# Reordering the modulation of the first norm in a two-sublayer decoder trunk

## The chip, the cores and the metric

The kernel runs on one core of one Trainium2 chip. The metric is the device time of one execution in microseconds, the median of several runs. TensorE is called PE here, VectorE DVE, ScalarE ACT, GpSimd POOL, and SP is the engine whose queue issues the DMAs.

## What is computed

One decoder layer on 1024 tokens of width 1024, in float32. A mixer sub-layer (three groups of heads) is followed by a gated feed-forward sub-layer and a final norm. Each sub-layer begins with an RMS norm that is scaled and shifted by a modulation: six vectors of 1024 that come from one product of the conditioning vector with a 1024 x 6144 matrix. The change is in the first of them.

```python
c_act = jax.nn.silu(c)
mod = c_act @ w_mod[l] + b_mod[l]
sh1, sc1, gt1, sh2, sc2, gt2 = [m[:, None, :] for m in jnp.split(mod, N_MOD, axis=-1)]
h = rms_norm(x, norm_mix[l]) * (1.0 + sc1) + sh1
p = h @ w_in[l]
...
x = x + gt1 * y
h = rms_norm(x, norm_ffn[l]) * (1.0 + sc2) + sh2
x = x + gt2 * conv_glu_ffn(h, ...)
return rms_norm(x, norm_final)
```

## The kernel before

Activations lie transposed: 128 of the 1024 channels on the partitions (a k tile, eight of them), 512 tokens along the free axis (a half f, two of them). A float32 product is made of three matmuls of a rounded format: a value is split into a high part `h` and a remainder `l` (ACT casts the high part, DVE or POOL subtracts for the remainder, `split` at L230), and h·h, h·l and l·h are summed.

**The stage around the change** (L411 to L454) makes h for the first 512 tokens. Its modulation comes in four groups m = 0 to 3; group m gives the shift and scale of the k tiles 2m and 2m+1 of h. A group's weights are four DMAs of 512 KB (`mod_load`, L336), tiles `wm` with two k tiles of 512 columns each. The product with the conditioning vector `cs` is spread over the engines: each of the eight k tiles is multiplied by its column of `cs` and added up. `mod_ap` (L343) does k 0 to 3: ACT multiplies, POOL adds, into the first sum `mb[m][0]`. `mod_v` (L350) does k 4 to 7 on DVE into the second sum `mb[m][1]`: one TENSOR_SCALAR and three SCALAR_TENSOR_TENSORs. `mod_fin` (L358) has PE sum both over the partitions (four one-column matmuls for each, tile `pm`), and DVE writes the result to `modc` (shift and scale) and `sg1` (scale plus one, times the norm's weight). Then `h_hi` (L372) multiplies x by `sg1` and by `rb`, the reciprocal root mean square of each token, and ACT adds the shift for the high part; `h_lo` (L380) is DVE's remainder. For k 0 to 3 DVE does both products at once; for k 4 to 7 POOL multiplies by `rb` (`xr`, L384) and DVE by `sg1`.

PE's products of the stage are three column tiles of the input projection, `pf0` to `pf2`; their weights `ws[0]` to `ws[2]` are split beside the modulation (`wh_s`, `wl_s`; the last remainder on POOL). Each takes 8 k tiles x 3 matmuls. `prod` (L400) emits those whose operands exist.

The order of the work is the order of the code, held fixed on DVE, ACT and POOL in this stage (`V.on`, `A.on`, `G.on`), and on PE while `T.on` is set. Before, group m's turn of the loop runs: ACT's and POOL's part of group m+1, the first two of DVE's four of group m+1, POOL's `xr`, `mod_fin(m)`, the matmuls of the first m weight tiles, `h_hi` of two k tiles, DVE's other two of group m+1, `h_lo`, and the split of weight tile m. An engine does its queue in order and waits at the first instruction that isn't ready.

After the stage ACT reads `pf0`, `pf1` and `pf2` (tiles `xwa`, `sgg`, `k`), PE goes on with the next column tile `pc_r`, and a chain of some 25 tiny operations (`spt`, L465 to L479) on POOL is followed there by `lol` (L490), which PE's product `pa` (L570) needs.

Of the kernel before, what the change touches and what calls it, by code (L numbers as in the profile page):

```python
# [10 lines left out]
F32 = mybir.dt.float32  # L11
# [7 lines left out]
P = 128  # L19
# [35 lines left out]
NF2 = 3  # L55
NT2, NTB, _ = 7, 9, 5
NWR, NWL, NH = 3, 2, 16
NAP, NXV, NFIRST, TON, XRO = (4, 4, 4, 4), 4, 3, True, ((4, 4), (4, 6), (6, 8), (8, 8))
VPIN = 0
ENG = {'s2':'G','KB1': 'V',  # L60
 'S1': 'V',
# [91 lines left out]
def trunk(ctx: ExitStack, tc: tile.TileContext, xT, wmod, w_in, w_out, w_up, w_down,  # L153
# [168 lines left out]
    def h_tile(f, k, x, rb, hl):  # L322
# [5 lines left out]
        V.scalar_tensor_tensor(lo, x, sh, hi.bitcast(F32), ALU.add, ALU.subtract)  # L328
        return hl

    acts = [[], []]
    first = {}
    with tc.tile_pool(name="st", bufs=1, reuse_waits="tile") as st:
        xs, ws = [], []

        def mod_load(m):  # L336
            for k2 in range(KT // 2):
                wt = st.tile([P, 2, H], F32, tag="wm", name=f"wm{m}_{k2}", bufs=6)
                SY.dma_start(wt, wmod[m, k2])
                wm[m] += [wt[:, 0, :], wt[:, 1, :]]  # L340
            mb[m] = [st.tile([P, H], F32, tag=f"mb{i}", name=f"mb{m}{i}", bufs=2) for i in range(2)]

        def mod_ap(m):  # L343
            a = mb[m][0]
            for k in range(NAP[m]):
                A.activation(wm[m][k] if k else a, wm[m][k], AF.Copy, scale=cs[:, k:k + 1])
                if k:
                    G.tensor_tensor(a, a, wm[m][k], ALU.add)

        def mod_v(m, k0, k1):  # L350
            a = mb[m][1]
            for k in range(max(k0, NAP[m]), k1):
                if k == NAP[m]:
                    V.tensor_scalar(a, wm[m][k], cs[:, k:k + 1], None, ALU.mult)
                else:
                    V.scalar_tensor_tensor(a, wm[m][k], cs[:, k:k + 1], a, ALU.mult, ALU.add)

        def mod_fin(m):  # L358
            ps = mp.tile([P, H], F32, tag="m", name=f"pm{m}")
            for n, a in enumerate(mb[m]):  # L360
                for i in range(4):
                    T.matmul(ps[:, i:i + 1], a[:, i * P:(i + 1) * P], ones, start=(n == 0 and i == 0), stop=(n == 1),
                             skip_group_check=True)
            V.tensor_tensor(modc[:, 4 * m:4 * m + 4], ps[:, 0:4], col("b_mod", 4 * m, 4), ALU.add)
            V.scalar_tensor_tensor(sg1[:, 2 * m:2 * m + 2], modc[:, 4 * m + 1:4 * m + 4:2], 1.0,
                                   col("norm_mix", 2 * m, 2), ALU.add, ALU.mult)

        def w_load(i):
            raw, hi, lo = ws[i]
            SY.dma_start(raw, w_in[i].rearrange("p k c -> p (k c)"))  # L370

        def h_hi(k):  # L372
            x, sh = xs[k], modc[:, 2 * k:2 * k + 1]
            if k < NXV:
                V.scalar_tensor_tensor(x, x, sg1[:, k:k + 1], rb, ALU.mult, ALU.mult)
            else:
                V.tensor_scalar(x, x, sg1[:, k:k + 1], None, ALU.mult)
            A.activation(hs[k][0], x, AF.Identity, bias=sh)

        def h_lo(k):  # L380
            V.scalar_tensor_tensor(hs[k][1], xs[k], modc[:, 2 * k:2 * k + 1], hs[k][0].bitcast(F32),
                                   ALU.add, ALU.subtract)

        def xr(k0, k1):  # L384
            for k in range(k0, k1):
                G.tensor_tensor(xs[k], xs[k], rb, ALU.mult)

        wm, mb = [[] for _ in range(4)], [None] * 4
        hs = [htile(f"h0{k}") for k in range(KT)]
        acts[0] += hs  # L390
        for i in range(NFIRST):
            raw = wp.tile([P, 1024], F32, tag="wraw", name=f"wr_s{i}", bufs=NWR)
            hi = st.tile([P, 1024], F32R, tag=f"wsh{i}", name=f"wh_s{i}")
            lo = st.tile([P, 1024], F32R, tag=f"wsl{i}", name=f"wl_s{i}")
            ws.append((raw, hi, lo))
            first[i] = acp.tile([P, H], F32, tag="acc", name=f"pf{i}")

        done = [0] * NFIRST

        def prod(k1, i1):  # L400
            for k in range(k1):
                ah, al = hs[k]
                for i in range(min(i1, NFIRST)):
                    if done[i] == k:
                        hi, lo = (t.rearrange("p (k c) -> p k c", c=P)[:, k, :] for t in ws[i][1:])
                        T.matmul(first[i], hi, ah, start=(k == 0), stop=False)
                        T.matmul(first[i], hi, al, start=False, stop=False)
                        T.matmul(first[i], lo, ah, start=False, stop=(k == KT - 1))
                        done[i] += 1

        V.on = A.on = G.on = True  # L411
        sacc = st.tile([P, H], F32, name="sacc0")
        for k in range(KT):
            xk = st.tile([P, H], F32, tag=f"x{k}", name=f"x0{k}")
            SY.dma_start(xk, xT[k * P:(k + 1) * P, 0:H])
            sq = st.tile([P, H], F32, tag="sq", name=f"sqx{k}", bufs=2)
            A.activation(sacc if k == 0 else sq, xk, AF.Square)
            if k:
                V.tensor_tensor(sacc, sacc, sq, ALU.add)
            xs.append(xk)  # L420
        mod_load(0)
        mod_load(1)
        mod_ap(0)
        rb = sumsq_bcast([sacc], mp, st, "rb", "n10", 1)
        mod_v(0, 0, 8)
        w_load(0)
        mod_load(2)
        w_load(1)
        mod_load(3)
        if NFIRST == 3:  # L430
            w_load(2)
        SY.dma_start(cst, const[:, 0:C_ID])
        lraw = wp.tile([P, 1024], F32, tag="wraw", name="lraw", bufs=NWR)[:, 0:768]
        SY.dma_start(lraw, lora.rearrange("p a b -> p (a b)"))
        for m in range(4):
            if m < 3:
                mod_ap(m + 1)
                mod_v(m + 1, 0, 6)
            xr(*XRO[m])
            T.on = TON  # L440
            mod_fin(m)
            if TON:
                prod(2 * m, m)
            T.on = False
            h_hi(2 * m)
            h_hi(2 * m + 1)
            if m < 3:
                mod_v(m + 1, 6, 8)
            h_lo(2 * m)
            h_lo(2 * m + 1)  # L450
            if m < NFIRST:
                split(*ws[m], eng(f"s{m}", "V"))
        prod(KT, NFIRST)
        V.on = A.on = G.on = False  # L454

# [32 lines left out]
    for i in range(2):  # L488
        r_, c_ = slice(64 * i, 64 * i + 64), slice(384 * i, 384 * i + 384)
        G.tensor_tensor(lol[r_, c_], lraw[r_, c_], lor[r_, c_].bitcast(F32), ALU.subtract)  # L490
    for i in range(NR):
        for t in (KGd, SCd, STd):
            G.memset(t[i], 0.0)
        if i < 2:
            G.memset(AKd[i][:, 0:4], 0.0)
            G.memset(AKd[i][:, 4:8], 0.0)
    g2s = r2.tile([P, 384], F32, name="g2s")
    SY.dma_start(g2s, g2w)
    lrw = r2.tile([P, 768], F32, name="lrw")
# [907 lines left out]
```

## Time and profile before

| | before |
|---|---|
| median of 3 runs | 1378.88 us (1377.09 to 1379.15) |
| the profiled execution, its own time | 1379.3 us |
| its span | 1377.5 us |
| PE busy | 1255.0 us (91% of the span) |
| DVE busy | 896.3 us (65%) |
| ACT busy | 583.7 us (42%) |
| POOL busy | 335.8 us (24%) |

The span is what the profiler sees of the program, the time is that of the execution around it. Busy time includes time in which an instruction has started and waits for something inside the engine, so a long DVE row can be a short one that was held up. The profile's chain of waits names only its longest pieces, the first of them at 747 us; for the first 75 us the engines' instructions are read one by one, in order of time.

### The profile page before, as it was taken

How to read it: one execution, taken by the hardware profiler on the slowest of the kernel's cores; microseconds unless marked ns; L12 is line 12 of the kernel's file. 1: busy time of each engine (PE TensorE's matmuls, PEld its weight loads, DVE VectorE, ACT ScalarE, POOL GpSimd, SP SyncE). 2: the span in 40 equal slices, each digit the busy share in tenths (PEclk: the TensorE clock that was granted, in tenths of full speed). 3: DMA queues.
4: the chain of work that ended last, by engine and by line, in shares of the span. 5: the costliest groups of instructions: out<-in, count | busy, mean ns of one | idle time of the engine just before them, and what ended most of it. 6: DMA issues, size and time to landing. Idle time of an engine off the chain costs nothing. (4 is left out here: it accounts for less than half of the span.)

```text
span 1377.5 us, 18630 instructions
## 1 busy us (share of the span) xinstructions
PE 1255.0 (91%) x6948; PEld 1026.9 (75%) x6948; DVE 896.3 (65%) x1667; ACT 583.7 (42%) x1008; POOL 335.8 (24%) x294
## 2 busy tenths in 40 slices
PE   3778999888998979999979899999999999999996
PEld 3566878667686767778757788888888888888885
DVE  6778765755668484467697766666566575432566
ACT  4364655854655366333363333434434342110231
POOL 6674423206125220000001433332333200000000
PEclk9899999979999997899998999999999999999998
DMA  7453251433314243296413322232222374321213
GB/s 283 156 169 100 56 165 54 120 117 85 83 48 112 63 121 116 86 301 204 129 61 99 100 82 72 84 92 84 91 67 81 126 249 138 88 78 52 80 54 122
DMA packets 87498, 153.89 MB, mean 112 GB/s; under 512 B 37616, under 2 KB 39280, under 8 KB 87408
## 3 DMA queue, kind: packets, MB, share of 16 engines
q1 hardware_dynamic: 87408, 152.71, 35.6%
q8 instruction: 54, 0.88, 0.3%
q14 instruction: 36, 0.29, 0.1%
HBM read 126.60 MB, written 26.08 MB: 111 GB/s over the span
## 5 line engine op out<-in xcount | busy, mean ns | idle before, releaser
L1249 DVE SCALAR_TENSOR_TENSOR x<-pd,modc,x 128x512 f32<-128x512 f32 x80 | 59.6, 749 | 85.4 <-PE pd L251 85.3
L290 POOL TENSOR_TENSOR macc<-macc,wm 128x512 f32<-128x512 f32 x35 | 47.1, 1345 | 67.9 <-ACT wm L288 65.7
L231 ACT CAST wh_wd<-wr_wd 128x768 fp32r<-128x768 f32 (+2 forms) x32 | 21.7, 678 | 95.9 <-PE pd L250 94.0
L1202 POOL TENSOR_TENSOR wr_uv<-wr_uv 128x512 f32<-128x512 f32 x3 | 4.5, 1516 | 227.4 <-DVE wr_ub L1201 227.4
L1296 POOL TENSOR_TENSOR x<-x,rb_n 128x512 f32<-128x512 f32 x2 | 3.0, 1515 | 217.3 <-ACT rb_n L273 217.3
L232 DVE TENSOR_TENSOR wl_ug<-wr_ug,wh_ug 128x1024 fp32r<-128x1024 f32 x22 | 26.9, 1224 | 38.9 <-ACT wh_ug L231 38.7
L1227 POOL TENSOR_TENSOR u<-u,g 128x512 f32<-128x512 f32 x21 | 27.7, 1321 | 92.8 <-ACT g L1150 92.8
L758 DVE TENSOR_SCALAR U<-q,rn 128x64 f32<-128x64 f32 x48 | 13.4, 279 | 48.9 <-PE q L746 41.7
L231 ACT CAST wh_ug<-wr_ug 128x1024 fp32r<-128x1024 f32 x22 | 23.2, 1054 | 48.3 <-PE pA L1125 35.6
L627 PE MATMUL pg<-KGd,KB 128*128 128x128 f32 x192 | 31.4, 309 | 8.4 <-DVE KGd L612 6.0
L766 ACT COPY O<-q 128x64 f32<-128x64 f32 x48 | 10.1, 210 | 66.4 <-PE q L746 66.1
L746 PE MATMUL q<-SS,KGd 128*128 128x64 f32 x180 | 37.2, 291 | 0.0
L1211 DVE TENSOR_TENSOR p<-p,pB 128x512 f32<-128x512 f32 x21 | 14.4, 686 | 34.9 <-PE pB L1126 34.9
L746 PE MATMUL q<-VV,SCd 128*128 128x64 f32 x192 | 35.5, 289 | 0.2
L627 PEld LDWEIGHTS pg<-KGd,KB 128*128 128x128 f32 x192 | 27.4, 216 | 9.9 <-DVE KGd L612 6.7
L1150 ACT ACTIVATE g<-g 128x512 f32<-128x512 f32 x44 | 27.9, 634 | 13.1 <-DVE g L1145 13.1
L746 PEld LDWEIGHTS q<-VV,SCd 128*128 128x128 f32 x192 | 30.3, 205 | 3.9 <-issue 1.1
L1143 DVE SCALAR_TENSOR_TENSOR g<-p,pr,g 128x511 f32<-128x511 f32 (+1 forms) x42 | 33.2, 790 | 0.0
L1143 DVE SCALAR_TENSOR_TENSOR g<-pA,pr,g 128x511 f32<-128x511 f32 (+1 forms) x42 | 31.2, 744 | 2.9 <-ACT g L1141 2.6
L288 ACT ACTIVATE wm<-wm,cs 128x512 f32<-128x512 f32 x35 | 24.1, 719 | 15.9 <-DMA wm<-in_wmod_dram 14.1
L1204 POOL TENSOR_TENSOR wr_ug<-wr_ug,wr_uv 128x512 f32<-128x512 f32 x18 | 29.9, 1663 | 1.4
L746 PEld LDWEIGHTS q<-SS,KGd 128*128 128x128 f32 x180 | 29.7, 207 | 0.5 <-issue 0.5
(5035 smaller groups left out, 4446.3 us busy)
## 6 DMA issues: line engine op xcount, KB each, us to landing
wm<-in_wmod_dram SPq DMA_DIRECT2D x48, 512.0 KB, 4.1
wr_ug<-in_w_up_dram SPq DMA_DIRECT2D x22, 512.0 KB, 3.6
wr_uv<-in_w_up_dram SPq DMA_DIRECT2D x22, 512.0 KB, 3.6
wr_g<-gd SPq DMA_DIRECT2D x22, 512.0 KB, 3.3
x<-in_xT_dram SPq DMA_DIRECT2D x32, 256.0 KB, 5.5
wr_wo<-in_w_out_dram SPq DMA_DIRECT2D x16, 512.0 KB, 4.2
wr_wd<-in_w_down_dram SPq DMA_DIRECT2D x16, 384.0 KB, 3.1
gd<-c SPq DMA_DIRECT2D x21, 256.0 KB, 2.0
```

Of the source, the lines that this page charges most:

```text
L231: A.copy(hi, src)
L232: (e or V).tensor_tensor(lo, src, hi.bitcast(F32), ALU.subtract)
L288: A.activation(acc if k == 0 else wt[:, j, :], wt[:, j, :], AF.Copy, scale=cs[:, k:k + 1])
L290: G.tensor_tensor(acc, acc, wt[:, j, :], ALU.add)
L627: T.matmul(pg[hh][:, c, :, :], KB[:, 4 * g + c, :, :].rearrange("p a b -> p (a b)"), KG[g][:, c, :, r_], start=True, stop=True)
L746: T.matmul(o, w, x, start=start, stop=True, skip_group_check=True)
L1143: V.scalar_tensor_tensor(g[:, d:H], src[:, 0:H - d], taps[2 - d], g[:, d:H], ALU.mult, ALU.add)
L1150: A.activation(g, g, AF.Silu)
L1204: eng("S4" + e, "G").tensor_tensor(g1, g1, v1, ALU.subtract)
L1211: V.tensor_tensor(self.p1, self.p1, psB, ALU.add)
L1227: eng("c22", "V").tensor_tensor(u3, u3, g1_, ALU.mult)
L1249: V.scalar_tensor_tensor(x, ps, modc[:, 40 + k:41 + k], x, ALU.mult, ALU.add)
```

## The change

The modulation is taken further ahead of h. ACT and POOL do the k tiles 1, 3 and 5 of each group, DVE does 0, 2, 4, 6 and 7 in one go. Groups 0 and 1 are done before the loop; in turn m ACT and POOL do group m+2, and DVE does group m+2 behind the two `h_lo` of group m and ahead of the split of weight tile m. `mod_fin(m+1)` stands between `h_hi` and `h_lo` of group m. POOL multiplies all eight k tiles by `rb`, and ACT takes DVE's product with `sg1`. The weights get eight buffers instead of six, and the zeroing of the rings (tiles `KGd`, `SCd`, `STd`, `AKd` of a later stage) moves to the top of the code.

```diff
-NAP, NXV, NFIRST, TON, XRO = (4, 4, 4, 4), 4, 3, True, ((4, 4), (4, 6), (6, 8), (8, 8))
+NFIRST = 3
+KAP_, KV_ = (1, 3, 5), (0, 2, 4, 6, 7)
...
+    for i in range(NR):
+        for t in (KGd, SCd, STd):
+            G.memset(t[i], 0.0)
+        if i < 2:
+            G.memset(AKd[i][:, 0:4], 0.0)
+            G.memset(AKd[i][:, 4:8], 0.0)
...
-                wt = st.tile([P, 2, H], F32, tag="wm", name=f"wm{m}_{k2}", bufs=6)
+                wt = st.tile([P, 2, H], F32, tag="wm", name=f"wm{m}_{k2}", bufs=8)
...
-            for k in range(NAP[m]):
-                A.activation(wm[m][k] if k else a, wm[m][k], AF.Copy, scale=cs[:, k:k + 1])
-                if k:
+            for k in KAP_:
+                first_ = k == KAP_[0]
+                A.activation(a if first_ else wm[m][k], wm[m][k], AF.Copy, scale=cs[:, k:k + 1])
+                if not first_:
                     G.tensor_tensor(a, a, wm[m][k], ALU.add)
...
-            for k in range(max(k0, NAP[m]), k1):
-                if k == NAP[m]:
+            for k in KV_[k0:k1]:
+                if k == KV_[0]:
...
-            if k < NXV:
-                V.scalar_tensor_tensor(x, x, sg1[:, k:k + 1], rb, ALU.mult, ALU.mult)
-            else:
-                V.tensor_scalar(x, x, sg1[:, k:k + 1], None, ALU.mult)
+            A.activation(x, x, AF.Copy, scale=sg1[:, k:k + 1])
...
-        mod_ap(0)
-        rb = sumsq_bcast([sacc], mp, st, "rb", "n10", 1)
-        mod_v(0, 0, 8)
...
+        mod_ap(0)
+        T.on = True
+        rb = sumsq_bcast([sacc], mp, st, "rb", "n10", 1)
+        T.on = False
+        mod_v(0, 0, 5)
+        fin(0)
+        mod_ap(1)
+        xr(0, 2)
+        mod_v(1, 0, 5)
         for m in range(4):
-            if m < 3:
-                mod_ap(m + 1)
-                mod_v(m + 1, 0, 6)
-            xr(*XRO[m])
-            T.on = TON
-            mod_fin(m)
-            if TON:
-                prod(2 * m, m)
-            T.on = False
+            if m + 2 < 4:
+                mod_ap(m + 2)
             h_hi(2 * m)
             h_hi(2 * m + 1)
-            if m < 3:
-                mod_v(m + 1, 6, 8)
+            if m + 1 < 4:
+                fin(m + 1)
+                xr(2 * m + 2, 2 * m + 4)
             h_lo(2 * m)
             h_lo(2 * m + 1)
+            if m + 2 < 4:
+                mod_v(m + 2, 0, 5)
             if m < NFIRST:
                 split(*ws[m], eng(f"s{m}", "V"))
+            T.on = True
+            prod(2 * m + 2, m + 1)
+            T.on = False
```

`fin(m)` is `mod_fin(m)` with PE's order held.

The change moves instructions on three engines; PE's and SP's orders stay. First DVE around the end of group 2 (`mb21` is DVE's sum of group 2, `mb31` that of group 3, `pm2` PE's sum of group 2 over the partitions, `wl_s0` and `wl_s1` the remainders of the first two weight tiles). Before:

```order
L149 TENSOR_TENSOR wl_s0_144<-wr_s0_142,wh_s0_143 128x1024
L149 TENSOR_SCALAR mb21_262<-wm2_2_257,cs_79 128x512
L149 SCALAR_TENSOR_TENSOR mb21_262<-wm2_2_257,cs_79,mb21_262 128x512
L149 TENSOR_TENSOR modc_76<-pm1_319,pr_66 128x4
L149 SCALAR_TENSOR_TENSOR sg1_77<-modc_76,pr_66 128x2
L149 SCALAR_TENSOR_TENSOR x02_164<-x02_164,sg1_77,rb_n10_246 128x512
L149 SCALAR_TENSOR_TENSOR x03_169<-x03_169,sg1_77,rb_n10_246 128x512
L149 SCALAR_TENSOR_TENSOR mb21_262<-wm2_3_259,cs_79,mb21_262 128x512 x2
L149 SCALAR_TENSOR_TENSOR h02l_131<-x02_164,modc_76,h02h_130 128x512
L149 SCALAR_TENSOR_TENSOR h03l_133<-x03_169,modc_76,h03h_132 128x512
L149 TENSOR_TENSOR wl_s1_148<-wr_s1_146,wh_s1_147 128x1024
L149 TENSOR_SCALAR mb31_273<-wm3_2_268,cs_79 128x512
```

With the change:

```order
L150 TENSOR_SCALAR mb21_237<-wm2_0_228,cs_79 128x512
L150 SCALAR_TENSOR_TENSOR mb21_237<-wm2_1_230,cs_79,mb21_237 128x512
L150 SCALAR_TENSOR_TENSOR mb21_237<-wm2_2_232,cs_79,mb21_237 128x512
L150 SCALAR_TENSOR_TENSOR mb21_237<-wm2_3_234,cs_79,mb21_237 128x512 x2
L150 TENSOR_TENSOR wl_s0_157<-wr_s0_155,wh_s0_156 128x1024
L150 TENSOR_TENSOR modc_76<-pm2_359,pr_66 128x4
L150 SCALAR_TENSOR_TENSOR sg1_77<-modc_76,pr_66 128x2
L150 SCALAR_TENSOR_TENSOR h02l_144<-x02_177,modc_76,h02h_143 128x512
```

Before, one operation more of `mb31` stands behind these rows, and then the read of `pm2` into `modc`: thirteen operations lie between it and `wl_s0`. With the change `wl_s0` stands behind all of group 2, and the read of `pm2` right behind `wl_s0`. The same holds for `wl_s1`, group 3 and `pm3`, except that the remainder of the next weight tile, `wl_r`, stands between the two.

On PE the order is the same in both; here it is with the change, around the same place (`pf0`, `pf1` are products of the first two weight tiles, `pm2` as above):

```order
L150 MATMUL pf0_158<-h00h_139,wl_s0_157 128x512
L150 MATMUL pf0_158<-h01h_141,wh_s0_156 128x512
L150 MATMUL pf0_158<-h01l_142,wh_s0_156 128x512
L150 MATMUL pf0_158<-h01h_141,wl_s0_157 128x512
L150 MATMUL pm2_359<-ones_74,mb20_236 128x1 x4
L150 MATMUL pm2_359<-ones_74,mb21_237 128x1 x4
L150 MATMUL pf1_162<-h00h_139,wh_s1_160 128x512
```

`pm2` stands behind four matmuls that need `wl_s0`, directly or by their place in the queue; in the same way `pm3` stands behind the matmuls of `pf1` that need `wl_s1`.

On POOL (`mb10` to `mb30` are POOL's sums of groups 1 to 3, `x00` and so on the k tiles of x), before:

```order
L149 TENSOR_TENSOR mb20_261<-mb20_261,wm2_0_253 128x512
L149 TENSOR_TENSOR mb20_261<-mb20_261,wm2_1_255 128x512 x2
L149 TENSOR_TENSOR x04_174<-x04_174,rb_n10_246 128x512
L149 TENSOR_TENSOR x05_179<-x05_179,rb_n10_246 128x512
L149 TENSOR_TENSOR mb30_272<-mb30_272,wm3_0_264 128x512
```

With the change:

```order
L150 TENSOR_TENSOR mb10_225<-mb10_225,wm1_1_219 128x512
L150 TENSOR_TENSOR mb10_225<-mb10_225,wm1_2_221 128x512
L150 TENSOR_TENSOR x00_168<-x00_168,rb_n10_283 128x512
L150 TENSOR_TENSOR x01_172<-x01_172,rb_n10_283 128x512
L150 TENSOR_TENSOR mb20_236<-mb20_236,wm2_1_230 128x512
L150 TENSOR_TENSOR mb20_236<-mb20_236,wm2_2_232 128x512
L150 TENSOR_TENSOR x02_177<-x02_177,rb_n10_283 128x512
L150 TENSOR_TENSOR x03_182<-x03_182,rb_n10_283 128x512
```

POOL has four operations for every group now, two adds and two products with `rb`, where it had three adds and at two of the groups two products more. None of them reads a result of DVE other than `rb`.

## Rows read from the trace of the kernel before

**Rows 1.** The view by stretches: busy time of each engine, PE clock, DMA.

```profile
30.00:40.00 10.00, 5.69 (x22) 4.43 (x22) 9.89 (x10) 4.16 (x7) 7.55 (x5) 0.95 0.95 366
40.00:50.00 10.00, 7.64 (x23) 6.34 (x24) 9.79 (x11) 4.12 (x6) 6.29 (x5) 0.53 0.54 189
50.00:60.00 10.00, 6.96 (x32) 5.56 (x31) 9.31 (x12) 4.66 (x8) 4.22 (x3) 0.83 0.18 52
```

Its columns are the stretch in us, its length, then the busy time (with the number of instructions) of PE, of PE's weight loads, of DVE, ACT and POOL, the granted PE clock as a share of full speed, the DMA share and GB/s.

**Rows 2.** The timeline of DVE: start, duration, line, operation, count, [idle before <-releaser].

```profile
19.28 0.48 DVE L149 TENSOR_SCALAR mb<-wm,cs 128x512 f32<-128x512 f32 x1
19.80 2.32 DVE L149 SCALAR_TENSOR_TENSOR mb<-wm,cs,mb 128x512 f32<-128x512 f32 x3
...
24.24 0.74 DVE L149 TENSOR_SCALAR mb<-wm,cs 128x512 f32<-128x512 f32 x1 [2.12 <-DMA wm<-in_wmod_dram]
...
34.65 1.64 DVE L149 SCALAR_TENSOR_TENSOR mb<-wm,cs,mb 128x512 f32<-128x512 f32 x1
...
36.40 1.03 DVE L149 SCALAR_TENSOR_TENSOR sg<-modc,pr 128x2 f32<-128x2 f32 x1
37.46 3.39 DVE L149 SCALAR_TENSOR_TENSOR x<-x,sg,rb_n 128x512 f32<-128x512 f32 x2
...
43.55 1.22 DVE L149 TENSOR_TENSOR wl_s<-wr_s,wh_s 128x1024 fp32r<-128x1024 f32 x1
...
59.14 0.75 DVE L149 SCALAR_TENSOR_TENSOR h07l<-x,modc,h07h 128x512 fp32r<-128x512 f32 x1
```

**Rows 3.** The timeline of POOL, 1 to 57 us.

```profile
1.23 0.95 POOL L493 MEMSET KGd<- 128x1024 f32 x1
...
13.75 3.96 POOL L149 TENSOR_TENSOR mb<-mb,wm 128x512 f32<-128x512 f32 x3 [0.75 <-ACT wm L149]
23.42 4.34 POOL L149 TENSOR_TENSOR mb<-mb,wm 128x512 f32<-128x512 f32 x3 [5.72 <-ACT wm L149]
32.29 5.12 POOL L149 TENSOR_TENSOR mb<-mb,wm 128x512 f32<-128x512 f32 x3 [4.53 <-ACT wm L149]
...
53.72 2.55 POOL L149 TENSOR_TENSOR wl_s<-wr_s,wh_s 128x1024 fp32r<-128x1024 f32 x1 [2.05 <-ACT wh_s L149]
```

**Rows 4.** The timeline of PE, 42 to 71 us.

```profile
42.36 1.87 PE L149 MATMUL pm<-ones,mb 128*128 128x1 f32 x8 [3.84 <-DVE mb L149]
...
45.52 0.63 PE L149 MATMUL pf<-h01h,wh_s 128*128 128x512 f32 x1
45.94 0.63 PE L149 MATMUL pf<-h01l,wh_s 128*128 128x512 f32 x1
...
50.03 0.39 PE L149 MATMUL pf<-h03h,wh_s 128*128 128x512 f32 x1
50.25 0.39 PE L149 MATMUL pf<-h03l,wh_s 128*128 128x512 f32 x1
...
53.45 1.05 PE L149 MATMUL pm<-ones,mb 128*128 128x1 f32 x8 [1.80 <-DVE mb L149]
...
68.17 0.39 PE L408 MATMUL pf<-h07h,wl_s 128*128 128x512 f32 x1
70.55 0.50 PE L249 MATMUL pc_r<-h00h,wh_r 128*128 128x512 f32 x1 [1.99 <-ACT cryC L541]
```

**Rows 5.** The timeline of ACT: products with a column, and the last h.

```profile
43.08 1.94 ACT L149 ACTIVATE wm<-wm,cs 128x512 f32<-128x512 f32 x3
...
58.35 0.71 ACT L149 ACTIVATE h07h<-x,modc 128x512 fp32r<-128x512 f32 x1
```

**Rows 6.** The timeline of POOL and PE behind the stage.

```profile
60.28 1.17 POOL L149 TENSOR_SCALAR spt<-spt 128x3 f32<-128x3 f32 x1 [4.01 <-ACT spt L149]
...
68.55 0.20 POOL L149 TENSOR_TENSOR spt<-spt 128x3 f32<-128x3 f32 x1
...
71.86 2.81 POOL L490 TENSOR_TENSOR lol<-lraw,lor 64x384 fp32r<-64x384 f32 x2
...
74.72 0.50 PE L570 MATMUL pa<-xwa,lol 128*128 128x512 f32 x1
```

More of the change, by code (lines that the diff above doesn't have):

```diff
@@ L434, in trunk, with fin @@
         SY.dma_start(lraw, lora.rearrange("p a b -> p (a b)"))
-        for m in range(4):
-            if m < 3:
-                mod_ap(m + 1)
-                mod_v(m + 1, 0, 6)
-            xr(*XRO[m])
-            T.on = TON
-            mod_fin(m)
-            if TON:
-                prod(2 * m, m)
-            T.on = False
+        def fin(m):
+            T.on = True
+            mod_fin(m)
+            T.on = False
[8 more added lines that the diff above has]
+        mod_v(1, 0, 5)
+        for m in range(4):
+            if m + 2 < 4:
+                mod_ap(m + 2)
             h_hi(2 * m)
             h_hi(2 * m + 1)
-            if m < 3:
-                mod_v(m + 1, 6, 8)
+            if m + 1 < 4:
+                fin(m + 1)
+                xr(2 * m + 2, 2 * m + 4)
             h_lo(2 * m)
             h_lo(2 * m + 1)
+            if m + 2 < 4:
+                mod_v(m + 2, 0, 5)
             if m < NFIRST:
                 split(*ws[m], eng(f"s{m}", "V"))
+            T.on = True
+            prod(2 * m + 2, m + 1)
+            T.on = False
         prod(KT, NFIRST)
@@ L490, in trunk @@
         G.tensor_tensor(lol[r_, c_], lraw[r_, c_], lor[r_, c_].bitcast(F32), ALU.subtract)
[L491 to L496, printed above, removed]
     g2s = r2.tile([P, 384], F32, name="g2s")
```

## The prediction

> **What bounds the kernel now.** I read the page's busy shares first: PE is busy for 91% of the span, so a stage in which PE is not full is where the order of the work matters. Then the view by stretches: from 30 to 60 us PE is busy for 5.7 to 7.6 us in 10, and DVE for 9.3 to 9.9 [rows 1]. So in this stage DVE is the engine that the others wait for, and the question is what its rows consist of. The timeline of DVE shows it: the same instruction, a modulation step of 128x512, takes 2.32 / 3 = 0.77 us while POOL rests and 1.64 us while POOL works; two products of x take 3.39 us [rows 2]. POOL's own operation takes 3.96 / 3 = 1.32 us while DVE does only tiny operations, and 5.12 / 3 = 1.71 us beside DVE [rows 3]. So where both have work, they take turns: about 1.68 us for one operation of each. The timeline of PE gives its prices: at the lower of its two clock levels (1.2 GHz) a matmul of 512 columns follows the last after 0.42 us and the eight records of one half of `pm` take 1.87 us; at the upper (2.4 GHz) 0.22 us and 1.05 us [rows 4]; the granted clock changes within the stage, 0.53 of full speed on average from 40 to 50 us [rows 1]. The stage ends at 68.56 us, the end of the last product of `pf`; `pc_r` begins at 70.55 [rows 4]. Behind that every engine works through its queue in the order before, each part waiting for the part ahead of it, so what the stage gains or loses I carry to the end unchanged.
>
> **The small parts.** *The rings:* POOL zeroes them from 1.23 us on in the kernel before already [rows 3], ahead of its first add, though the code stood far below. Nothing moves: 0. *Eight weight buffers:* DVE idles 2.12 us for a weight tile at 24.24 [rows 2]; with eight buffers both tiles of group 1 that were late are issued behind the other six. This gap goes, but a longer wait stands in its place (step 2 below). *ACT's new products:* a product with a column goes every 1.94 / 3 = 0.65 us [rows 5]; ACT has four fewer of the weights' and eight more of x, +2.6 us on an engine that is busy 4.1 to 4.7 us in 10 [rows 1]: hidden until the last two k tiles, counted there. *DVE's work:* eight products of x go, four steps of 0.77 us come; POOL has sixteen operations before and after.
>
> **The stage, laid out in the new order.** Each engine's queue is followed from where the two traces must still agree, DVE's first modulation step at 19.28 [rows 2], with an operation starting when its engine is free and its inputs are there.
>
> 1. Group 0 on DVE: 0.48 + 4 x 0.78 -> 22.9.
> 2. The read of `pm0` comes next. PE needs 1.87 us for the second half -> 24.8, and 0.2 us until DVE has read it. The step behind it, `sg`, took 1.03 us beside POOL [rows 2]: 26.1. DVE stood still for 2 us.
> 3. Group 1 on DVE: five steps. POOL starts its adds at 23.42 [rows 3] and now has eight operations in a row (two adds, two products of x, and the same again) that need nothing of DVE's but `rb`. So all five go at 1.68 us: 34.5. Then `pm1`: 1.87 us, another stop, 36.8 with `sg`.
> 4. `h00l`, `h01l`, and group 2: POOL works on the adds of group 3 and then its last four products, until about 45. The two remainders go beside one add: 39.2. Four steps at 1.65: 45.8, the fifth alone: 46.5. `wl_s0`, 1.22 us [rows 2]: 47.75. Up to here eleven operations of DVE are held up by POOL.
> 5. **The hand-over.** DVE now reads `pm2`. In PE's queue `pm2` stands behind four matmuls that waited for `wl_s0`: 4 x 0.42 + 2 x 1.7 (the pairs overlap) + 0.2 -> 53.2; DVE idles 5.5 us. Before, `wl_s0` was long done and `pm2` complete when DVE came to it. `sg` is ready at 53.6.
> 6. `h02l`, `h03l` and group 3, with POOL's `wl_s2` of 2.55 us [rows 3] in the way: 1.4 + 3.6 + 2.2 -> 60.8; `wl_s1` 1.22 -> 62.0. Before, it was done at 43.55 + 1.22 = 44.8 [rows 2].
> 7. The second hand-over: sixteen matmuls stand between `wl_s1` and `pm3`. The first ten or so go at the lower clock, as in all such restarts here (0.42 us at 45.52 [rows 4], three us after PE's idle time of 3.84): 4.4 + 1.4, then `pm3` 2 x 1.0: 69.8, and `sg` 70.5. DVE does `wl_r` meanwhile and idles about 6 us.
> 8. ACT makes the last two k tiles, four instructions of 0.65 us and a start: h07h ends at 73.3, where it ended at 59.06 [rows 5]. DVE's last remainder: 74.3, from 59.9 [rows 2].
> 9. PE has 48 matmuls left behind `pm3`: 48 x 0.225 = 10.8 -> 80.6.
>
> **The sum.** 80.6 against 68.56: 12.0 us later. On the other way out of the stage, ACT's tiny operations behind h07h start POOL's chain `spt`, with `lol` behind it, which PE's `pa` takes at once at 74.72 [rows 6]: 15.6 us from h07h to `lol`. It begins 14.2 us later and loses two hold-ups of about 0.9 us by DVE's splits (1.17 us at 60.28 for three columns, where such an operation takes 0.20 [rows 6]): `lol` 12.4 us later. Both ways say +12. The profiled execution took 1379.3 us, so 1391.3; the median of the runs, 1378.88, is 0.4 us lower, so I say 1391.
>
> **The rule against the trace.** The rows show two held-up engines taking turns at 1.68 us for a pair whose parts take 0.77 + 1.32 = 2.09 us apart [rows 2, 3], and I have used 1.68. The Trainium skill ("SBUF — State Buffer", section "Who interferes with whom") states that a DVE instruction with two SBUF inputs and a GpSimd instruction that reads SBUF block each other fully, for the whole instruction. By that a pair would cost the whole 2.09 us, and the eleven pairs of steps 2 to 4 would make it 1395.5; the trace agrees that they exclude each other, not that nothing overlaps.
>
> **Bounds.** What no row of before shows is the clock of PE in the two hand-overs, since PE now rests 10 us and more ahead of each. If it is the upper one throughout, step 5 shortens by 4 x 0.2 + 2 x 0.7 = 2.2 us and step 7 by 10 x 0.2 = 2.0: 1387. If it stays low for half of step 9 as well, 24 x 0.2 = 4.8 us more, and `pm3` 1.7: 1397.5. Slack behind the stage could swallow some 2 us. That gives 1384 to 1398.
>
> **Rivals.** *A, faster: DVE's total decides, and the hand-overs are covered.* Before, DVE is full from 30 to 60 us [rows 1]. Were the new waits for `pm1`, `pm2` and `pm3` each under a microsecond, only the work would count: eight operations of DVE go and four come, so four fewer at 0.77 to 1.70 us [rows 2], 3 to 7 us less, 1374 in the middle. The place is DVE's three reads of `pm`; the point is whether PE has finished `pm2` when DVE is through `wl_s0`. For it speaks that POOL's and ACT's parts of group 2 are ready 10 us earlier than DVE's; against it, that PE's queue puts four matmuls with `wl_s0` ahead, which nothing covers. 0.07. *B, no change: the time is given back behind the stage.* PE waits 1.99 us for ACT there [rows 4], and further waits may stand in the rest of the mixer; were they for something that doesn't hang on the stage, some 10 of the 12 us could vanish: 1381. But the weights' DMAs wait for buffers that the stage's own splits free. 0.05. *C, slower, by the turns alone:* the matmuls of `pf` that stand before `pm2` and `pm3` cost nothing, since PE runs them earlier; `pm2` then follows group 2 at once and step 5 falls by 4.7 us (46.5 + 1.9 + 0.5 = 48.9); step 7 falls by 2 only, since `wl_r`, whose weights can be fetched only behind `wl_s1`, holds DVE: 1384.5. POOL's run of operations is then what is lost. For it speaks that `wh_s0` is early; against it, that the third matmul needs `wl_s0`. 0.13. *Forecast,* with its clock variants: 0.75.
>
> **The numbers.** The time is the forecast's, 1391. The range 1384 to 1398 takes in the forecast with its bounds and C, 0.88 in all; what is left out is A, B and a little of the clock's tail. A measurement of this kernel tells about 0.2% (2.8 us) from no change. Slower by more than that: the forecast and C, 0.88; within it: B, 0.05; faster: A, 0.07.
>
> **What would show it.** In the profile of the changed kernel the timeline of DVE should show idle time ahead of three reads of `pm`, ended by PE: about 2 us near 36, 5 to 6 us near 53, and again some 6 us near 70. DVE's steps of group 1 should read 1.6 to 1.7 us each. `wl_s1` should end near 62, h07h near 73, the last product of `pf` near 81, and `pa` near 87. DVE's busy time from 30 to 60 us should fall below 9 in 10. If the reads of `pm2` and `pm3` follow their predecessors at once, steps 5 and 7 are wrong; if they are there and the time is nevertheless near 1380, the carrying to the end is.

## The result and the profile after

The changed kernel took 1392.18 us in the median of 4 runs (1386.95 to 1395.33), the kernel before 1377.99 us beside it: a ratio of 1.0102, 95% interval 1.0069 to 1.0135. It is slower, by 14.2 us in the medians.

| | before | after |
|---|---|---|
| the profiled execution, its own time | 1379.3 us | 1394.47 us |
| its span | 1377.5 us | 1392.7 us |
| PE busy | 1255.0 us | 1261.9 us |
| DVE busy | 896.3 us | 893.3 us |
| ACT busy | 583.7 us | 588.4 us |
| POOL busy | 335.8 us | 334.3 us |

No engine's work changed by more than 7 us; what changed is when it is done. The view by stretches of the changed kernel, with the columns of [rows 1], shows where:

```profile
30.00:40.00 10.00, 3.29 (x10) 2.28 (x10) 7.90 (x9) 7.51 (x10) 9.92 (x7) 1.00 0.74 263
40.00:50.00 10.00, 3.18 (x11) 2.80 (x12) 6.66 (x5) 0.00 (x0) 4.29 (x3) 1.00 0.14 40
50.00:60.00 10.00, 3.16 (x12) 2.44 (x12) 7.69 (x10) 3.71 (x5) 2.34 (x1) 1.00 0.00 1
```

Before, DVE was busy for 9.3 to 9.9 us in 10 here [rows 1]; now for 6.7 to 7.9, and PE's 5.7 to 7.6 have become 3.2 or 3.3. An engine that was the bound has become one that waits. What for stands in DVE's timeline (start, duration, line, operation, count, idle before and its releaser):

```profile
18.73 0.48 DVE L150 TENSOR_SCALAR mb<-wm,cs 128x512 f32<-128x512 f32 x1
19.25 3.11 DVE L150 SCALAR_TENSOR_TENSOR mb<-wm,cs,mb 128x512 f32<-128x512 f32 x4
24.32 0.16 DVE L150 TENSOR_TENSOR modc<-pm,pr 128x4 f32<-128x4 f32 x1 [1.96 <-PE pm L150]
...
27.04 6.66 DVE L150 SCALAR_TENSOR_TENSOR mb<-wm,cs,mb 128x512 f32<-128x512 f32 x4
35.65 0.16 DVE L150 TENSOR_TENSOR modc<-pm,pr 128x4 f32<-128x4 f32 x1 [1.96 <-PE pm L150]
...
39.87 5.76 DVE L150 SCALAR_TENSOR_TENSOR mb<-wm,cs,mb 128x512 f32<-128x512 f32 x4
45.55 1.22 DVE L150 TENSOR_TENSOR wl_s<-wr_s,wh_s 128x1024 fp32r<-128x1024 f32 x1
52.13 0.16 DVE L150 TENSOR_TENSOR modc<-pm,pr 128x4 f32<-128x4 f32 x1 [5.37 <-PE pm L150]
...
59.25 1.21 DVE L150 TENSOR_TENSOR wl_s<-wr_s,wh_s 128x1024 fp32r<-128x1024 f32 x1
67.12 1.23 DVE L233 TENSOR_TENSOR wl_r<-wr_r,wh_r 128x1024 fp32r<-128x1024 f32 x1 [6.66 <-ACT wh_r L232]
68.27 0.15 DVE L150 TENSOR_TENSOR modc<-pm,pr 128x4 f32<-128x4 f32 x1
68.45 0.16 DVE L150 SCALAR_TENSOR_TENSOR sg<-modc,pr 128x2 f32<-128x2 f32 x1
```

The four reads of `pm` (into `modc`) are where DVE stands: 1.96, 1.96 and 5.37 us; the fourth gap, 6.66 us, is booked on `wl_r`, one instruction ahead of the read. PE's timeline shows the other half of the hand-over:

```profile
46.82 0.79 PE L150 MATMUL pf<-h00h,wl_s 128*128 128x512 f32 x1 [9.23 <-DVE wl_s L150]
47.41 0.63 PE L150 MATMUL pf<-h01h,wh_s 128*128 128x512 f32 x1
47.84 0.63 PE L150 MATMUL pf<-h01l,wh_s 128*128 128x512 f32 x1
...
48.69 3.41 PE L150 MATMUL pm<-ones,mb 128*128 128x1 f32 x16
...
60.52 0.79 PE L150 MATMUL pf<-h00h,wl_s 128*128 128x512 f32 x1 [7.36 <-DVE wl_s L150]
...
66.08 1.84 PE L150 MATMUL pm<-ones,mb 128*128 128x1 f32 x16
...
78.58 0.39 PE L150 MATMUL pf<-h07h,wl_s 128*128 128x512 f32 x1
80.35 0.50 PE L250 MATMUL pc_r<-h00h,wh_r 128*128 128x512 f32 x1 [1.38 <-ACT cryC L551]
```

PE waits for DVE's split (9.23 and 7.36 us), then DVE waits for PE's sum: while one works, the other stands. The last product of `pf` ends at 78.58 + 0.39 = 78.97 us, before at 68.56 [rows 4]: 10.4 us later. POOL's way out of the stage is as late:

```profile
71.98 0.52 POOL L150 TENSOR_SCALAR spt<-spt 128x3 f32<-128x3 f32 x1 [13.20 <-ACT spt L150]
...
82.00 2.63 POOL L506 TENSOR_TENSOR lol<-lraw,lor 64x384 fp32r<-64x384 f32 x2
```

`lol` ends at 84.63, before at 74.67 [rows 6]: 10.0 us later. From there one group of PE's products was followed, the sixteen into `pmx` near 200 us, and one matmul some 20 us behind it. Before, and then after:

```profile
198.13 1.09 PE L915 MATMUL pmx<-swT,sv 128*64 128x128 f32 x16
...
217.57 0.39 PE L251 MATMUL pc_r<-h04h,wl_r 128*128 128x512 f32 x1
```

```profile
208.74 1.09 PE L925 MATMUL pmx<-swT,sv 128*64 128x128 f32 x16
...
233.67 0.40 PE L252 MATMUL pc_r<-h04h,wl_r 128*128 128x512 f32 x1
```

At `pmx` the changed kernel is 10.6 us late, as at the stage's end: the delay was carried. At the second row it is 16.1 us late. The stretches from 220 us on, before and after, say why:

```profile
220.00:225.00 5.00, 5.00 (x35) 4.46 (x33) 3.58 (x8) 2.31 (x5) 0.00 (x0) 1.00 0.01 3
```

```profile
220.00:225.00 5.00, 5.00 (x42) 3.62 (x41) 1.62 (x2) 3.15 (x5) 0.04 (x1) 0.50 0.01 3
```

The granted clock was at its lower level here, 0.50 of full speed (1.2 GHz). So of this profiled execution's 15.2 us, 10.6 were there at `pmx`, and some 5 came with a stretch of lower clock far behind the stage.

### The profile page after: what moved, and what is told of

It is laid out like the page before. It is cut to its first block, busy times and chain, and to the rows that moved or that the text cites. A ratio compares the mean times of both kernels' runs of the same rounds, so it can differ in the third digit from the quotient of the medians.

```text
span 1392.7 us, 18638 instructions
## 1 busy us (share of the span) xinstructions
PE 1261.9 (91%) x6948; PEld 1032.6 (74%) x6948; DVE 893.3 (64%) x1663; ACT 588.4 (42%) x1012; POOL 334.3 (24%) x294
```

## The experiments

Theory H: the loss is the hand-over. DVE's splits `wl_s0`, `wl_s1` come behind a whole group now, PE's sums `pm2`, `pm3` stand behind products that need them, and DVE's next step behind the sums. Rival T: DVE and POOL taking turns is the loss. Theory K: whatever the stage loses is carried to the end; rival S: it is swallowed. The kernel before was run again beside each set: 1376.64 us (35 runs) beside split_first, pm_first, no_rb and small_parts, 1375.8 (28) beside changed_again, x_alone, delay_only and pe_direct, 1377.07 (23) beside pe_direct2 and rings_held. Since a median moves by a few us with things that lie behind the stage, the stage is read in the profile. This table has the start of four rows in each profile; the time is the median's difference from the kernel before beside it.

| kernel | h07h | last pf | lol | pmx | time | ratio, 95% |
|---|---|---|---|---|---|---|
| before | 58.35 | 68.17 | 71.86 | 198.13 | | |
| changed | 70.84 | 78.58 | 82.00 | 208.74 | +14.2 | 1.0069 to 1.0135 |
| changed_again | 71.66 | 79.68 | 82.86 | 208.77 | +13.1 | 1.0059 to 1.0113 |
| split_first | 62.52 | 70.56 | 75.15 | 201.38 | +2.5 | 1.0013 to 1.0044 |
| pm_first | 59.14 | 73.70 | 75.14 | 200.59 | +1.3 | 0.9997 to 1.0025 |
| no_rb | 65.40 | 73.49 | 76.62 | 202.27 | +3.6 | 1.0015 to 1.0047 |
| small_parts | 57.65 | 68.51 | 71.16 | 199.35 | -2.1 | 0.9978 to 1.0006 |
| x_alone | 63.81 | 71.20 | 75.25 | 202.30 | +5.7 | 1.0020 to 1.0059 |
| delay_only | 70.28 | 76.24 | 81.46 | 208.55 | +8.7 | 1.0033 to 1.0077 |
| pe_direct | 59.63 | 67.65 | 73.20 | 200.02 | +4.1 | 1.0002 to 1.0051 |
| pe_direct2 | 53.68 | 61.67 | 67.19 | 193.55 | +1.1 | 0.9989 to 1.0033 |
| rings_held | 58.88 | 68.98 | 72.38 | 199.21 | +1.0 | 0.9989 to 1.0022 |

### split_first: the split ahead of the group

```diff
-            if m + 2 < 4:
-                mod_v(m + 2, 0, 5)
             if m < NFIRST:
                 split(*ws[m], eng(f"s{m}", "V"))
+            if m + 2 < 4:
+                mod_v(m + 2, 0, 5)
```

> The changed kernel, with one swap: in each turn DVE does the split of the weight tile (wl_s0, wl_s1) ahead of its five steps of the next-but-one group, not behind them. Nothing else moves; POOL, PE and SP keep their orders. Theory H (the loss is the hand-over: pm2 and pm3 stand in PE's queue behind matmuls that wait for a split which now comes late): wl_s0 ends near 41, wl_s1 near 52, the reads of pm2 and pm3 follow within 2 us, h07h ends near 64, and the stage's last pf product near 70 instead of 78.97; the time falls by about 9 us to some 1380 to 1385, near the kernel before. Rival T (the loss is DVE and POOL taking turns because POOL has an unbroken run of operations): the number of held-up operations is the same, so the gaps only change place, and the time stays within 3 us of the changed kernel's 1392.

1379.13 us (1377.28 to 1385.88): 2.5 us over its kernel before, where the changed kernel is 13 to 14 over. DVE's timeline:

```profile
38.42 2.29 DVE L150 TENSOR_TENSOR wl_s<-wr_s,wh_s 128x1024 fp32r<-128x1024 f32 x1
...
49.00 0.16 DVE L150 TENSOR_TENSOR modc<-pm,pr 128x4 f32<-128x4 f32 x1 [1.96 <-PE pm L150]
...
50.60 1.22 DVE L150 TENSOR_TENSOR wl_s<-wr_s,wh_s 128x1024 fp32r<-128x1024 f32 x1
...
59.94 0.16 DVE L150 TENSOR_TENSOR modc<-pm,pr 128x4 f32<-128x4 f32 x1 [2.59 <-PE pm L150]
```

`wl_s0` ends at 40.71, `wl_s1` at 51.82, and the waits for `pm2` and `pm3` are 1.96 and 2.59 us in place of 5.37 and 6.66. The last `pf` product starts 8.0 us earlier, as theory H said; the wait for `pm3` is a little over its 2 us and the time 1 us under its range. One thing moved that the expectation left out: `wl_r` is outside the fixed order, and it now stands behind the read of `pm3`.

### pm_first: the sums ahead of the products

```diff
             if m + 1 < 4:
                 fin(m + 1)
+                T.on = True
+                prod(2 * m, m)
+                T.on = False
                 xr(2 * m + 2, 2 * m + 4)
...
-            T.on = True
-            prod(2 * m + 2, m + 1)
-            T.on = False
         prod(KT, NFIRST)
```

> The changed kernel with PE's order altered alone: the matmuls of pf that become possible in a turn are put behind the next group's sum pm, so that pm2 and pm3 no longer wait for wl_s0 and wl_s1. DVE, ACT, POOL and SP keep their orders, so DVE's split of the weight tile is as late as in the changed kernel. Theory H: DVE's gap of 5.37 us ahead of the read of pm2 falls to 2 us or less, the one at pm3 is bounded only by what DVE does between; sg of group 3 comes about 6 us earlier, the last pf product 5 to 7 us earlier, though PE has more matmuls left at the end: 1384 to 1388. Rival T: what PE does first doesn't matter, DVE is late by its own held-up steps: within 2 us of 1392.

1377.90 us (1372.11 to 1380.26), 6 us below the expectation. DVE's timeline, with the split as late as in the changed kernel:

```profile
45.37 1.22 DVE L150 TENSOR_TENSOR wl_s<-wr_s,wh_s 128x1024 fp32r<-128x1024 f32 x1
47.41 0.16 DVE L150 TENSOR_TENSOR modc<-pm,pr 128x4 f32<-128x4 f32 x1 [0.82 <-PE pm L150]
...
54.53 1.21 DVE L150 TENSOR_TENSOR wl_s<-wr_s,wh_s 128x1024 fp32r<-128x1024 f32 x1
56.57 0.16 DVE L150 TENSOR_TENSOR modc<-pm,pr 128x4 f32<-128x4 f32 x1 [0.82 <-PE pm L150]
```

Both waits fall to 0.82 us, h07h is back to within 0.8 us of the kernel before, though every turn with POOL is still there. That is the plainest sign that the queue's order made most of the loss up to h07h. The stage's end is 4.9 us earlier, just under the expected 5 to 7 (PE has more products left), but the expectation took PE's end for what carries. POOL's way carries: `lol` is only 3.3 us later than before, and `pmx` 2.5. As in split_first, `wl_r` and `wl_v` moved behind the remainders of h, so this run takes away two things ahead of `pm3`: PE's order, and the wait of `wl_r` for its weight. The wait for `pm2` has only the first. The two ahead of `pm3` were not tried apart.

### no_rb: POOL without its products

```diff
         def xr(k0, k1):
             for k in range(k0, k1):
-                G.tensor_tensor(xs[k], xs[k], rb, ALU.mult)
+                pass
```

> The changed kernel without POOL's eight products x*rb (the multiplication of the first norm's x by the reciprocal root mean square is left out for the first 512 tokens), so POOL's unbroken run shrinks to two adds per group. Theory H: DVE's steps become quicker where POOL no longer takes turns (about six of them by 0.9 us), but both hand-overs stay, with PE's gaps ahead of wl_s0 and wl_s1 still several us: 4 to 6 us less, 1386 to 1388. Rival T (the turns are the whole loss): the whole 10 us of the stage come back, 1380 to 1382.

This run leaves the multiplication by `rb` out. 1380.23 us (1377.52 to 1385.34): rival T's number, but not its account. DVE's timeline still has both hand-overs:

```profile
39.86 1.22 DVE L150 TENSOR_TENSOR wl_s<-wr_s,wh_s 128x1024 fp32r<-128x1024 f32 x1
46.45 0.16 DVE L150 TENSOR_TENSOR modc<-pm,pr 128x4 f32<-128x4 f32 x1 [5.37 <-PE pm L150]
...
60.58 1.23 DVE L233 TENSOR_TENSOR wl_r<-wr_r,wh_r 128x1024 fp32r<-128x1024 f32 x1 [5.81 <-ACT wh_r L232]
```

5.37 us again, to the hundredth. What fell is the time up to `wl_s0`, 46.77 to 41.08, by the turns; the stage ends 5.1 us earlier, theory H's 4 to 6, `lol` 5.4 and `pmx` 6.5. So POOL's products are a part of the loss and not the whole of it: at the stage's end no more than some half of the 10.4 us, since this run takes out also the four that POOL had before. Over their kernels before, the median fell by 9.5 to 10.6 us (3.6 against 13.1 and 14.2); what more than the 6.5 of `pmx` it holds lies behind the stage and is open. The median alone would have voted for T.

### small_parts: buffers and rings alone

```diff
-                wt = st.tile([P, 2, H], F32, tag="wm", name=f"wm{m}_{k2}", bufs=6)
+                wt = st.tile([P, 2, H], F32, tag="wm", name=f"wm{m}_{k2}", bufs=8)
```

with the zeroing of the rings moved to the top as in the change.

> The kernel before with the two small parts of the change alone: eight weight buffers instead of six, and the rings zeroed at the top of the code. Theory H and rival T alike: the rings change nothing, the 2.12 us for which DVE waits for a weight tile at 24 us go, but the same time is lost again in front of pm0 or in the turns, so the time is that of the kernel before within 2 us, 1376 to 1380. If it is slower than 1382, a part of the loss is in the buffers or the rings, and both theories are short of it.

1374.59 us (1373.04 to 1377.47): no difference that counts. The stage ends 0.3 us later than before, as expected, although DVE's wait for a weight tile at 24 us [rows 2] is gone.

### x_alone: the products of x alone

```diff
-NAP, NXV, NFIRST, TON, XRO = (4, 4, 4, 4), 4, 3, True, ((4, 4), (4, 6), (6, 8), (8, 8))
+NAP, NXV, NFIRST, TON, XRO = (4, 4, 4, 4), 4, 3, True, ((0, 2), (2, 4), (4, 6), (6, 8))
...
-            if k < NXV:
-                V.scalar_tensor_tensor(x, x, sg1[:, k:k + 1], rb, ALU.mult, ALU.mult)
-            else:
-                V.tensor_scalar(x, x, sg1[:, k:k + 1], None, ALU.mult)
+            A.activation(x, x, AF.Copy, scale=sg1[:, k:k + 1])
```

> The kernel before, with one part of the change alone: POOL multiplies all eight k tiles of x by rb, and ACT takes DVE's product with sg1. DVE has eight operations fewer, POOL four more, ACT eight more; the groups of the modulation, the splits and PE stay in their old order. Theory H (orders, not the amount of work, made the loss; but POOL's four products more cost DVE some turns and ACT's products are on the way at the last k tiles): the stage's last pf product ends 2 to 4 us later than before, 1379 to 1381. Rival T (moving the products to POOL is the loss): 8 us or more. Rival W (DVE's work is the bound, and it has less): 3 us or more faster.

1381.54 us (1376.93 to 1386.40). The last `pf` product starts 3.0 us later than before, theory H's 2 to 4, and the median is 0.5 us above its 1381. Giving DVE less to do made nothing faster (rival W). Rival T's 8 us did not come, but the move alone is slower by 5.7 us, and its cause is not one of the changed kernel. POOL's `wl_s2` with its last two products behind it, and ACT, which waits for the first of them:

```profile
56.45 2.35 POOL L149 TENSOR_TENSOR wl_s<-wr_s,wh_s 128x1024 fp32r<-128x1024 f32 x1 [2.67 <-ACT wh_s L149]
58.76 2.53 POOL L149 TENSOR_TENSOR x<-x,rb_n 128x512 f32<-128x512 f32 x2
60.07 0.72 ACT L149 ACTIVATE x<-x,sg 128x512 f32<-128x512 f32 x1 [3.70 <-POOL x L149]
```

In the changed kernel POOL is through all eight products at 37.84 + 6.46 = 44.30 us, ahead of `wl_s2`:

```profile
37.84 6.46 POOL L150 TENSOR_TENSOR x<-x,rb_n 128x512 f32<-128x512 f32 x4
```

DVE's read of `pm3` was even 0.6 us earlier than before. So this run doesn't price the move as the change makes it.

### delay_only: the delay without the change

```diff
             T.on = TON
+            if m == 3:
+                dly = st.tile([P, H], F32, name="dly")
+                for _ in range(14):
+                    V.tensor_tensor(dly, xs[0], xs[1], ALU.add)
             mod_fin(m)
```

> The kernel before, with 14 additions of 128x512 on DVE that nobody reads, placed ahead of its read of pm3. They go one after another about every 0.67 us, so DVE reads pm3 some 9 us later, and with it come the last two k tiles of h, the last product of pf and POOL's chain spt. Nothing else of the change is there: no run-ahead, no turns with POOL, no late split. Theory K (what the stage loses is carried to the end, and a stretch of lower clock near 205 to 232 us, which moves when the work before it moves, adds up to 5 us): the last pf product ends 8 to 9 us later, near 77, everything to 200 us shifts by as much, and the time is 8 to 14 us over the kernel before. Rival S (the mixer has slack that swallows such a delay, so the changed kernel's loss comes from something else as well): the time rises by less than 5 us.

1384.50 us (1380.07 to 1390.84). DVE's read of `pm3` came at 68.67 us in place of 56.74, 11.9 us later and not 9, since the splits `wl_r` and `wl_v` went in between the additions; the last `pf` product starts 8.1 us later. `lol` starts 9.6 us later than before, `pmx` 10.4, and the time is 8.7 us more (interval 4.5 to 10.6): theory K. Most of a delay of this size at the end of the stage reaches the end of the program, without anything else of the change. The stretch of lower clock, which the expectation had counted in, did not come.

### changed_again: the change once more

No edit.

> The changed kernel itself, on the same chip as the runs beside it, to have its time and its stretch of lower clock near 218 to 232 us once more. Theory K: the stage's last pf product ends at 79 again and the whole is 10 to 15 us over the kernel before; the lower clock near 220 us is there again, since it belongs to when the work arrives there. If it is gone and the time is 10 us over, that stretch is chance. Rival: under 8 us over, so that a part of the first measurement was the chip.

1388.90 us (1383.45 to 1392.18), 13.1 us over the kernel before. `pmx` is 10.6 us late, as in the first profile, but the clock did not fall there:

```profile
220.00:225.00 5.00, 4.99 (x52) 3.63 (x52) 3.37 (x4) 4.88 (x11) 0.62 (x1) 1.00 0.28 105
```

So that stretch does not belong to when the work arrives there, and the first part of the expectation failed. The row of `pc_r` that the first profile had at 233.67 us is 6.5 us earlier here:

```profile
227.17 0.39 PE L252 MATMUL pc_r<-h04h,wl_r 128*128 128x512 f32 x1
```

This profiled execution took 1385.14 us, the first 1394.47, with the same 10.6 us at `pmx`.

### pe_direct and pe_direct2: a version meant to beat both

From split_first: PE takes k tiles 1, 3 and 5 of each group itself, DVE makes the first four products of x.

```diff
+                for i in range(4):
+                    T.matmul(ps[:, i:i + 1], wm[m][k][:, i * P:(i + 1) * P], cs[:, k:k + 1],
+                             start=(n == 0 and i == 0), stop=False, skip_group_check=True)
```

> A version that is meant to beat both, built on the changed kernel: the split stands ahead of the run-ahead group on DVE; the k tiles 1, 3 and 5 of every group, which ACT multiplied and POOL added, are taken by PE itself (one-column products of the weights with cs, twelve for a group, summed in pm); and DVE makes the first four products of x at once as in the kernel before, POOL and ACT the last four. So POOL has four operations in the stage and a split, where it had sixteen, and DVE is seldom held up. Theory H: DVE's steps read 0.77 us throughout, wl_s0 ends near 37, wl_s1 near 46, h07h near 56, the last pf product near 64 to 66, 3 to 5 us ahead of the kernel before: 1372 to 1375. Rival: PE's twelve columns more for each group stand ahead of the pf products at the lower clock and cost 2.8 us each, and the time is that of the kernel before within 3 us.

1379.88 us (1373.23 to 1389.17): 4.1 us over its kernel before, and neither theory H's 1372 to 1375 nor the rival's 3 us. Ahead of the stage the profile has something new, in DVE's timeline:

```profile
2.85 10.06 DVE L197 TENSOR_SCALAR omu<-pr 128x11 f32<-128x11 f32 x1 [2.85 <-DMA pr<-in_par_dram]
...
3.14 9.80 DVE L205 TENSOR_SCALAR hka<-pr 128x3 f32<-128x3 f32 x1
12.97 0.17 DVE L207 TENSOR_SCALAR oka<-hka 128x3 f32<-128x3 f32 x1
```

DVE's tiny operations stood for 10 us, until POOL's run of zeroing ended (its last row, 0.95 us from 11.93). The stage began 4 us late; the last `pf` product still started 0.5 us earlier than before, but `lol` 1.3 us later. pe_direct2 takes that away (its zeroing waits for `cs`, the last three pieces stand behind `rb` in the code) and moves PE's columns of group 0 (`mod_pe`) forward:

```diff
+    G.on = True
+    G.tensor_scalar(STd[0].rearrange("p a b c -> p (a b c)")[:, 0:8], cs, 1.0, None, ALU.mult)
...
+        mod_pe(0)
+        T.on = True
+        rb = rstd_bcast(pss, mp, st, "rb", "n10", 1)
```

> pe_direct with two things mended that its profile shows: POOL's zeroing of the rings begins only when the conditioning vector cs is there (in that profile DVE's tiny operations ahead of cs stood from 2.85 to 12.9 us, until POOL's run of zeroing ended), and PE takes the twelve columns of group 0 between the sum of squares and the broadcast of rb, not behind it. Theory H: DVE's first modulation step starts near 19.3 instead of 23.1, pm0 is read near 25 instead of 31.9, h07h ends near 55, the last pf product near 63; carried, 3 to 5 us under the kernel before, 1371 to 1373. Rival: with POOL's zeroing lasting to 17 us the rsqrt's tiny operations on DVE are held up in its place, and the clock of PE stays low through its columns: within 2 us of the kernel before.

The first of these operations now takes 0.17 us; the last `pf` product starts at 61.67 and `lol` at 67.19, 6.5 and 4.7 us ahead of the kernel before. The profiled execution took 1373.78 us, 5.5 less than that of before. But the median of 12 runs is 1378.14 (1373.75 to 1385.21): no difference that can be shown, and theory H's 1371 to 1373 is missed. The profiled execution was the second fastest of the twelve, that of before is 2.6 us over its median of 35, so the 5.5 us flatter the version. Why nothing of the stage's gain shows in the median is open.

### rings_held: the zeroing held back

The first two lines of the last diff, put into small_parts ahead of the zeroing.

> small_parts (the kernel before with eight buffers and the rings zeroed at the top) and one tiny operation of POOL ahead of the zeroing that reads the conditioning vector cs, so POOL's run of zeroing can't begin before DVE's tiny operations for cs are done. If the 10 us for which DVE stood in pe_direct's profile come now and then in every kernel, the slowest runs go and the spread of 12 runs is below 5 us, with the median unchanged or 1 us lower (1373 to 1376); on the other side the zeroing now ends near 17 us and POOL's adds of group 0 come 3 us later, which the wait for rb hides. If it belongs to pe_direct alone, nothing changes: small_parts' 1374.6 within 1.5 us. If the later adds are not hidden, 2 to 3 us slower than small_parts.

1378.06 us, 12 runs from 1375.26 to 1381.83. Neither of the first two readings holds: the spread of 6.6 us is not under 5, and the median is 3.5 us over small_parts (3.0 when each is taken against the kernel before beside it). The third, that the later adds are not hidden, isn't shown either: `lol` is 1.2 us later (72.38 against 71.16), but `pmx` 0.1 earlier. So the spread of the runs isn't POOL's zeroing alone; whether the 10 us of pe_direct come now and then in every kernel is open.

## Why the prediction was right

1391 us was predicted, 1392.18 measured, inside the likeliest case. Step by step, each end as forecast and as measured in the profile after:

| step | forecast | measured |
|---|---|---|
| 1 group 0 on DVE | 22.9 | 22.36 |
| 2 `pm0`, `sg` | 26.1 | 25.51 |
| 3 group 1; `pm1`, `sg` | 34.5; 36.8 | 33.70; 36.08 |
| 4 group 2; `wl_s0` | 46.5; 47.75 | 45.63; 46.77 |
| 5 first hand-over, `sg` | 53.6 | 52.49 |
| 6 group 3, `wl_s1` | 62.0 | 60.46 |
| 7 second hand-over, `sg` | 70.5 | 68.61 |
| 8 h07h | 73.3 | 71.56 |
| 9 last `pf` | 80.6 | 78.97 |

DVE began at 18.73 where 19.28 was assumed, 0.55 us; the rest, about 1.1 us, comes in pieces of at most 0.45 a step.

*The turns* (steps 3 and 4) are as said: four DVE steps beside POOL in 6.66 us, 1.67 each, where 1.68 was taken. The rule that was weighed against it is one of the Trainium skill ("SBUF — State Buffer", section "SBUF: two separate sides"): of a DVE instruction with two SBUF inputs and a GpSimd instruction that reads SBUF, the one that starts first gets the shared port pair for the whole instruction, and the other fully blocks. By that rule the rows' 0.77 + 1.32 us would make an estimated 2.09 us for the two; the trace agrees that they take turns, and the measurement decides for 1.67. *The first hand-over* was 5.37 us for 5.5, and pm_first shows that PE's order made it. (The terms of step 5 add up to 53.0, not the 53.2 that it goes on with.) *The second* has the right length, but the prediction's sign for it failed: the gap is ended by ACT's cast `wh_r`, not by PE. The fetch of the weight `wr_r` was issued at 60.5 us, when `wl_s1` had ended at 60.46 and freed its buffer, and landed 5.5 us later: the point that rival C had raised. ACT's timeline:

```profile
66.05 1.05 ACT L232 CAST wh_r<-wr_r 128x1024 fp32r<-128x1024 f32 x1 [9.68 <-DMA wr_r<-in_w_in_dram]
```

PE's sums ended at 66.08 + 1.84 = 67.92 and `wl_r` at 68.35: two waits behind the same late split, within half a microsecond of each other. Either alone would have held DVE until then. In changed_again the weight came earlier, and there the second wait is PE's, as the sign had said:

```profile
66.51 1.23 DVE L233 TENSOR_TENSOR wl_r<-wr_r,wh_r 128x1024 fp32r<-128x1024 f32 x1 [5.90 <-ACT wh_r L232]
69.08 0.16 DVE L150 TENSOR_TENSOR modc<-pm,pr 128x4 f32<-128x4 f32 x1 [1.34 <-PE pm L150]
```

*The sum* was 12.0 us, and the stage cost 10.4 (10.0 by `lol`, where 12.4 was said), 11.5 in changed_again's profile. The term that was missing is behind the stage: the medians are 14.2 and 13.1 us over, about 3 more than the 10.6 that arrive at `pmx`. In the first profile the stretch of lower clock near 220 us adds to it; changed_again has no such stretch, and its profiled execution was only 5.8 us over that of before. So two errors of opposite sign, 0.5 to 1.6 us too much in the stage and some 3 too little behind it, made the hit closer than the working was: that the time came within 1.2 us is luck. *Carried to the end* holds to a few microseconds only. From `pmx` to the end, the four profiles with that stretch lost another 1.9 to 5.8 us to the profile of before, and the seven others won back 0.9 to 4.8. Were the stretch commoner in the changed kernel's executions than in those of the kernel before, the missing 3 us would be there; with one profile for each kernel, or two, that isn't shown.

Of the rivals, A (covered hand-overs) and B (given back) are out, A by the gaps, B by `pmx` and the medians. C (the turns alone) is out by the 5.37 us and by pm_first, but its remark on `wl_r` was right, and the turns are no small part: the start of the last `pf` product came forward by 5.1 us without POOL's products, by 8.0 with the split first and by 4.9 with the sums first. These overlap and don't add up to a sum. The small parts cost nothing, as small_parts shows.

## What to carry to other kernels

When work is run ahead on one engine, look at what it is put in front of: here a split of 1.2 us moved behind five steps, and in the next engine's queue everything that nobody had meant to delay stood behind that split. Before moving such an operation, read both queues together, and give the short operation that another engine waits for its place first. Judge an experiment on one stage by the rows at that stage's end and on each way out of it, and only then by the median: here two medians of one kernel differ by up to 3.3 us, as much as several of these versions move the stage.

## What was not expected of the hardware

- In pe_direct's profile five tiny DVE operations lasted until the end of POOL's unbroken run of zeroing, 10.06 us, where the longest of them took 1.0 to 1.3 us in nine other profiles with the same run of zeroing, and 0.17 us in the two where it was held back.
- The granted clock read 1.00 from 30 to 60 us in the changed kernel, while PE's matmuls there followed one another every 0.43 us, as at its lower level; before, the same column showed 0.53 at such a pace [rows 1, 4]. So the pace has to be read from the rows.
- A stretch of lower clock appeared between 210 and 235 us in four of the twelve profiles (changed, split_first, no_rb and pe_direct; 0.50 to 0.66 at its lowest in slices of 5 us) and not in the other eight, changed_again among them. What PE did before it sets the four apart: it begins during the 64 small matmuls into `pz` or soon behind them, and ahead of these PE had stood still for 1.31, 2.01, 2.07 and 2.26 us in the four, for at most 1.07 in the others. Changed, split_first and before:

```profile
215.88 0.72 PE L703 MATMUL pz<-X,AKd 16*32 16x16 f32 x64 [1.31 <-issue]
```

```profile
209.22 0.72 PE L703 MATMUL pz<-X,AKd 16*32 16x16 f32 x64 [2.01 <-DVE X L708]
```

```profile
205.04 0.72 PE L693 MATMUL pz<-X,AKd 16*32 16x16 f32 x64 [1.07 <-issue]
```

  That the wait brings the clock down is not shown, since no run lengthened it on purpose; why it is longer in some executions is open.
